# Grouped-query attention on one core: new planner constants, a reordered start, a shared last product

## The chip, the cores and the metric

The kernel runs on one core of a Trainium2 chip. The metric is the device time of one execution in microseconds, as the median of several runs. Five engines work side by side on a core: TensorE (PE in the profile, its weight loads PEld), VectorE (DVE), ScalarE (ACT), GpSimd (POOL) and SyncE (SP), which here only issues DMAs. Each engine takes its own instructions in order and waits on semaphores for the others.

## The reference

For each of 8 batches and 8 query heads, with 2 heads of keys and values (4 query heads share one), 1024 positions and 64 features:

```python
scores = scale * np.matmul(q_group, k_group.transpose(0, 1, 3, 2))
scores_max = np.max(scores, axis=-1, keepdims=True)
attn = np.exp(scores - scores_max)
attn = attn / (np.sum(attn, axis=-1, keepdims=True) + 1e-08)
output[:, q_start:q_end, :, :] = np.matmul(attn, v_group)
```

That is 64 jobs (a batch and a query head each), every one with 1024 x 1024 exponentials.

## The kernel before

**The work of a job.** The scores are made transposed, keys on the partitions. A job has 8 chunks of 128 keys; a chunk is a pair of matmuls (L522) into one PSUM slot of 128 x 1024 floats. There are three such slots (`sps`), each of two banks. The two matmuls of a pair use different halves of the rows of the array, and which key block goes with which half is why each turned k (`kt`) has a second plane with its halves swapped. From the slot the exponential goes to SBUF in bf16, by one of two ways:

- ScalarE takes the chunk with one ACTIVATE (L532, tile `pt`): 384 of the 512 chunks.
- VectorE takes it with an approximation in integer arithmetic: `yt` (L543, one pass over PSUM per chunk), and then for two chunks together `zt` (L550), `et` (L557) and a product (L566). For all jobs but the last two, `et` and `zt` both enter the next product (so such a chunk costs TensorE one more matmul per output piece); for the last two they are added (L571). This is a "chain"; 128 chunks make 64 of them.

The second product (L584) has 8 pieces per job, each of 128 queries, and accumulates 8 to 10 matmuls of 128 x 65 in PSUM; column 65 is the sum of the row, since v has a column of ones. Seven pieces share a bank (`PB = 7`), then VectorE takes the reciprocal of the sums (`rec`, L630) and multiplies (L633, tile `ost`), and SP stores whole jobs (L642). The last job is different: its chunks are accumulated as they come (`pvl`, L605) into both banks of a spare slot, four pieces in each, and each half is normalized and stored by itself (`half`, L617; the first half's store is issued by SP, the second's by ScalarE).

**The order.** Nothing is ordered by hand. The class `Plan` simulates TensorE, ScalarE and VectorE with cost constants (`M_...`, in ns), and writes a list of events; the kernel emits its instructions in that order. Since each engine takes its instructions in order, the plan decides only the order, not the times. The rules that matter here:

- `pick_d` (L88): VectorE may take at most `MXD = 2` chunks of a job, of the job in hand or the next two whose q is there.
- A score for ScalarE (kind "A") is emitted when ScalarE's planned work ahead (`runway`) is about to run out (`slack <= M_GAP`), or earlier, when a second slot is free or TensorE is at scores anyway and the runway is under `M_RUNWAY`. At most two are queued.
- Otherwise TensorE does `GRAIN = 3` matmuls of the second product at a time, and then decides again. Changing between scores and the second product costs `M_SWITCH`.
- In score mode TensorE may wait up to `M_WAIT` for a slot to come free rather than switch.
- Loads and turns of q, k and v, and the stores, are put into the event list at fixed distances from the planned times.

**The start (L412 to L454).** SP loads k of the first pair of heads and then v, ScalarE's queue loads q, GpSimd casts the q of the next jobs to bf16 in DRAM. TensorE runs 6 matmuls of 512 columns on zeros (`dummy`). k is cast by VectorE (L433), q by ScalarE (L434); TensorE turns k (four matmuls), then q (four), then the swapped k (eight, L445). VectorE copies the first block of k out (L450), ScalarE all of q (L451), VectorE the rest of k (L452) and the swapped plane (L453). The first score needs L450 and L451.

**Buffers.** `pt` has 32 buffers. So that the reuse of a buffer needs no wait of its own, every twelfth exponential is made to wait for the exponential 15 before it (L534 to L537).

Of the kernel before, what the change touches and what calls it, by code (L numbers as in the profile page):

```python
# [8 lines left out]


M_START = 5450
M_SWAP = 1200
M_Q1 = 3500
M_QSTEP = 2700
M_WARM = 7000
M_FILL = 12000
M_DUMMY = 110
M_SEE = 51
M_PAIR = 226
M_PTAIL = 205  # L20
M_SWITCH = 92
M_MM = 33.5
M_PVTAIL = 180
M_ACT = 905
M_ATAIL = 135
M_FIX = 76
M_DTAIL = 83
M_DEP = 34
M_D1 = 1.042
M_D2 = 0.521  # L30
M_D4 = 0.261
M_REC = 115
M_GAP = 60
M_RUNWAY = 1500
M_BACK = 2500
M_WAIT = 200
STEP = 10
INF = float("inf")
PB = 7
NPIECE = 8  # L40
GRAIN = 3
MXD = 2
TAIL = 2
STEPS = (("zh", M_D4), ("two", M_D4), ("mul", M_D2), ("add", M_D2))


class Plan:


    def __init__(self, nj, npt, nct, nyt):  # L50
        self.nj, self.npt, self.nct, self.nyt = nj, npt, nct, nyt
        self.ev = []
        self.spare = None
        self.mms = [8] * nj

        self.last = (nj - 1) * NPIECE
        self.groups = [(i, min(i + PB, self.last)) for i in range(0, self.last, PB)]
        self.groups += [(self.last, self.last + 4), (self.last + 4, self.last + 8)]
        self.group_of = [g for g, (lo, hi) in enumerate(self.groups) for _ in range(lo, hi)]
        self.run()  # L60

    def run(self):
        nj, ev = self.nj, self.ev
# [23 lines left out]

        def pick_d():  # L88
            for j in range(a, min(nj, a + 3)):
                if todo[j] and dcount[j] < MXD and qready[j] <= tP:  # L90
                    return j
            return None

        while pc < last or steps or norms:
# [12 lines left out]
            if tD == t:  # L107
# [27 lines left out]
                else:  # L135
# [10 lines left out]
                    if best:  # L146
                        at = max(t, dend + M_DEP) if best[0] else t
                        ch = best[2]
                        if ch is None:
                            _, _, lo, hi = norms.pop(0)  # L150
                            ev.append((t, "norm", (lo, hi), None, None))
                            end = at + M_FIX + 64 * (hi - lo) * M_D1
                            out_free[group_of[lo] % 2] = end + M_DTAIL + M_SEE
                            dlast = None
                        else:
                            n = len(ch["pairs"])
                            kind, rate = ch["steps"][ch["at"]]
                            ev.append((t, kind, None, ch["id"], n))
                            end = at + M_FIX + 1024 * n * rate
                            ch["at"] += 1  # L160
                            dlast = (ch["id"], ch["at"])
                            if ch["at"] == len(ch["steps"]):
                                chains.remove(ch)
                                for j, c in ch["pairs"]:
                                    p_ready[j][c] = end + M_DTAIL + M_SEE
# [82 lines left out]
            elif (  # L248
# [14 lines left out]
                ev.append((tP, "pvl", c, len(steps), None))  # L263
                tP += NPIECE * M_MM
                if not steps:
                    norms.append((tP + M_PVTAIL - 100, "rec", last, last + 4))
                    norms.append((tP + M_PVTAIL, "rec", last + 4, last + 8))
            elif t < M_FILL and pc == 0 and done == 0:
                ev.append((tP, "dummy", None, None, None))
                tP += M_DUMMY  # L270
# [13 lines left out]
def kernel(  # L284
# [28 lines left out]
    NPT = 32  # L313
# [99 lines left out]
    b16 = {x: kvp.tile([128, NH, 2 * D], BF16, name=f"{x}16") for x in "kq"}  # L413
    kt[(0, 0)] = ktp.tile([128, 2, HS], BF16, name="kt")
    qt[0] = qp.tile([128, 1, HS], BF16, name="qt")
    nc.sync.dma_start(out=f32["k"], in_=rows(k[0, 0], True))
    nc.scalar.dma_start(out=f32["q"], in_=rows(q[0, 0], True))
    load_v(0, 0)
    cast_q(1)
    make_identity(nc, ident)  # L420
    cast_q(2)
# [7 lines left out]
                ops[1][:, 0:cols], lhsT=warm[:, 0:128], rhs=warm[:, 0:cols], start=True, stop=True  # L429
            )  # L430

    dummy(6, HS)
    nc.vector.tensor_copy(out=b16["k"], in_=f32["k"])  # L433
    nc.scalar.activation(out=b16["q"], in_=f32["q"], func=AF.Copy)  # L434
    turned = {"k": new_slot(2)[:, 0, :], "q": new_slot(1)[:, 0, :]}
    for x in "kq":
        for c in range(NH):
            nc.tensor.matmul(  # L438
                turned[x][:, c * 128 : (c + 1) * 128],
                lhsT=b16[x][:, c, :], rhs=ident, start=True, stop=True,  # L440
            )
    for c in range(NH):
        for half in range(2):
            lo = half * D
            nc.tensor.matmul(  # L445
                ops[0][lo : lo + D, c * 128 : (c + 1) * 128],
                lhsT=b16["k"][:, c, D - lo : 2 * D - lo], rhs=ident, start=True, stop=True,
            )
    k0 = kt[(0, 0)]
    nc.vector.tensor_copy(out=k0[:, 0, 0:128], in_=turned["k"][:, 0:128])  # L450
    nc.scalar.activation(out=qt[0][:, 0, :], in_=turned["q"], func=AF.Copy)  # L451
    nc.vector.tensor_copy(out=k0[:, 0, 128:HS], in_=turned["k"][:, 128:HS])  # L452
    nc.vector.tensor_copy(out=k0[:, 1, :], in_=ops[0])  # L453
    turn_q(1)  # L454
    ev = list(plan.ev)
    n = len(ev)
# [15 lines left out]
    for x in [e for e in plan.ev if e[1] == "norm"]:  # L472
        lo, hi = x[2]
        for j in range(NJ - 1):
            if lo < (j + 1) * NPIECE <= hi:
                ev.append((x[0] + 700, "store", None, j, None))
        if lo >= plan.last:
            ev.append((x[0] + 1, "half", (lo, hi), None, None))
    order = {id(e): i for i, e in enumerate(ev)}
    ev.sort(key=lambda e: (e[0], order[id(e)]))  # L480

# [17 lines left out]
    for when, kind, x, j, c in ev:  # L499
# [14 lines left out]
        elif kind == "score":  # L514
# [4 lines left out]
            for half in range(2):  # L519
# [6 lines left out]
                    start=True,  # L526
                    stop=True,
                )
        elif kind == "act":
            p = pp.tile([128, 2, HS], BF16, name="pt")  # L530
            pt[(j, c)] = p
            exps.append(nc.scalar.activation(out=p, in_=where_s[(j, c)], func=AF.Exp, scale=scale))  # L532

            if len(exps) % 12 == 0 and len(exps) > 16:  # L534
                tc.add_manual_dep(
                    exps[-1].ins, exps[-16].ins.name, Sync, reason="buffers written before"
                )  # L537
        elif kind == "dpass":
            ch, i = j
# [72 lines left out]
                    )  # L612
        elif kind == "half":
            b, h = divmod(NJ - 1, H)
            lo, hi = x
            i = (lo - plan.last) // 2
            (nc.scalar if i else nc.sync).dma_start(  # L617
                out=rows(out[b, h])[:, i : i + 2],
                in_=ost[:, lo % RING : lo % RING + 4, :].rearrange("p (s two) d -> p s (two d)", two=2),
            )  # L620
        elif kind in ("rec", "norm"):
            lo, hi = x
            n = hi - lo
            o = ops[plan.group_of[lo] % 2]
            if lo >= plan.last:
                o = sps[plan.spare][:, (lo - plan.last) // 4, :]
            o = o[:, 0 : n * (D + 1)].rearrange("p (s d) -> p s d", d=D + 1)
            if kind == "rec":
                rec = rp.tile([128, PB], FP32, name="rec")
                nc.vector.reciprocal(out=rec[:, 0:n], in_=o[:, :, D])  # L630
            else:
                r = lo % RING
                nc.vector.tensor_tensor(  # L633
                    out=ost[:, r : r + n, :],
                    in0=o[:, :, 0:D],
                    in1=rec[:, 0:n].unsqueeze(2).to_broadcast([128, n, D]),
                    op=ALU.mult,
                )
        elif kind == "store":
            b, h = divmod(j, H)  # L640
            r = j * NPIECE % RING
# [35 lines left out]
```

The softmax here doesn't subtract the row's maximum and nothing guards it: scores larger than these inputs give would overflow.

## Time and profile before

| what | value |
|---|---|
| median of 6 runs | 366.65 us (365.76 to 368.26) |
| the profiled execution | 367.02 us |
| its span, first to last instruction | 365.2 us |
| TensorE / VectorE / ScalarE / GpSimd busy | 346.1 / 351.6 / 355.1 / 50.9 us |
| granted TensorE clock | 1.000 |
| exponentials on ScalarE, L532 | 384, 352.6 us busy |
| passes on VectorE over PSUM, L543 | 128, 155.7 us busy |
| matmuls of scores, L522 / of the second product, L584 | 1024 / 5024 |
| DMA, mean | 123 GB/s |

The profiled execution lies 0.37 us over the median, and 1.8 us of its time lie outside its span. A busy time counts each instruction from its start to its last write, and on ScalarE and VectorE one starts before the one ahead has ended; so a mean per instruction (1.10 us for an exponential) is more than what an instruction adds, which is the distance from start to start. On TensorE a pair of scores shows up as 0.384 us each, though the two run together.

### The profile page before, as it was taken

To read this page: it belongs to the slowest core of one execution; us is meant where nothing else is said; L and a number is where in the kernel's file an instruction comes from. 1 tells how busy PE (TensorE), PEld (TensorE's weight loads), DVE (VectorE), ACT (ScalarE), POOL (GpSimd) and SP (SyncE) were. 2 spreads that over 40 slices of the span, in tenths; PEclk is the share of its full clock that TensorE was granted. 3 is DMA by queue.
4 is the path that set the end of the run, shared out by engine and by line. 5 is a ranking of instruction groups with operands and counts; after the bars stand their busy time and mean duration, and the time that the engine had idled before them with its cause. 6 is when DMAs were issued, how large, how long until landed. Compare 5 with 4: busy or idle time off the path is not lost.

```text
span 365.2 us, 13795 instructions
## 1 busy us (share of the span) xinstructions
PE 346.1 (95%) x6155; PEld 220.4 (60%) x6155; DVE 351.6 (96%) x476; ACT 355.1 (97%) x387; POOL 50.9 (14%) x100
## 2 busy tenths in 40 slices
PE   6899999999999999999999999999999999999995
PEld 3466666666666666666656666655666656666664
DVE  3999999999999999999999999999999999999993
ACT  4999999999999999999999999999999999999994
POOL 3112021021211112021111112102111111211000
PEclk9999999999999999999999999999999999999999
DMA  5544768568647665857669576669686548754223
GB/s 154 92 102 115 133 118 147 131 117 162 117 89 155 124 145 92 171 100 132 149 103 157 105 140 138 120 145 117 110 158 114 139 85 170 131 120 91 70 59 88
DMA packets 89164, 44.81 MB, mean 123 GB/s; under 512 B 45488, under 2 KB 87345, under 8 KB 87857
## 3 DMA queue, kind: packets, MB, share of 16 engines
q1 hardware_dynamic: 86192, 33.31, 39.8%
q0 software_dynamic: 2496, 10.23, 21.8%
q8 instruction: 48, 0.79, 1.0%
q10 hardware_dynamic: 416, 0.39, 0.4%
q14 instruction: 12, 0.09, 0.1%
HBM read 25.17 MB, written 27.00 MB: 143 GB/s over the span
## 4 chain that ended last, share of the span: by engine, by line
ACT 56%; DVE 37%; PE 3%; DMA 1%; issue 1%
ACT pt L532 56%; DVE yt L543 16%; DVE zt L566 8%; DVE zt L550 5%; DVE ost L633 4%; DVE et L557 4%; PE sp L522 1%; DMA k<-in_k_dram 1%; DVE rec L630 1%; PE ops L584 1%; PE sp L605 1%; PE sp L438 0%; PE ops L428 0%; ACT qt L451 0%; DVE k L433 0%
## 5 line engine op out<-in xcount | busy, mean ns | idle before, releaser
L532 ACT ACTIVATE pt<-sp 128x1024 bf16<-128x1024 f32 x384 | 352.6, 1101 | 1.0 <-PE sp L522 0.7
L522 PE MATMUL sp<-qt,kt 64*128 64x512 bf16 x1024 | 173.3, 384 | 12.3 <-ACT pt L532 6.9
L584 PE MATMUL ops<-va,pt 128*128 128x65 bf16 x3024 | 184.6, 194 | 0.0
L584 PEld LDWEIGHTS <-pt 128*128 128x128 bf16 x3024 | 135.8, 97 | 43.2 <-issue 43.2
L543 DVE TENSOR_SCALAR yt<-sp 128x1024 uint16<-128x1024 f32 x128 | 155.7, 1217 | 2.3 <-PE sp L522 1.9
L584 PE MATMUL ops<-va,zt 128*128 128x65 bf16 x1008 | 124.4, 194 | 0.0
L584 PE MATMUL ops<-va,et 128*128 128x65 bf16 x992 | 120.3, 194 | 0.0
L584 PEld LDWEIGHTS <-et 128*128 128x128 bf16 x992 | 80.3, 98 | 26.0 <-issue 26.0
L584 PEld LDWEIGHTS <-zt 128*128 128x128 bf16 x1008 | 83.2, 97 | 6.9 <-issue 6.9
L522 PEld LDWEIGHTS <-kt 64*128 64x128 bf16 x1024 | 47.4, 93 | 58.0 <-issue 36.9
L566 DVE TENSOR_TENSOR zt<-yt,zt 128x2048 bf16<-128x2048 bf16 x64 | 78.0, 1219 | 0.0
L359 POOL DMA_DIRECT2D qd<-in_q_dram x63 | 32.5, 516 | 214.8 <-PE sp L522 208.6
L550 DVE TENSOR_SCALAR zt<-yt 128x2048 uint16<-128x2048 uint16 x64 | 46.4, 724 | 0.1
L633 DVE TENSOR_TENSOR ost<-ops,rec 128x448 f32<-128x448 f32 x72 | 44.2, 614 | 0.0
L557 DVE TENSOR_SCALAR et<-yt 128x2048 uint16<-128x2048 uint16 x64 | 43.2, 675 | 0.0
L367 POOL DMA_DIRECT2D kd<-in_k_dram x15 | 7.3, 487 | 64.9 <-PE sp L522 60.1
L630 DVE RECIPROCAL rec<-ops 128x7 f32<-128x7 f32 x72 | 14.1, 196 | 1.4 <-PE ops L584 1.3
L384 POOL CAST va<-vs 128x512 bf16<-128x512 f32 x16 | 10.6, 662 | 0.3 <-DMA vs<-in_v_dram 0.3
L428 PE MATMUL ops<-warm 128*128 128x128 bf16 (+1 forms) x27 | 4.7, 328 | 1.2 <-DVE warm L351 1.2
L428 PEld LDWEIGHTS <-warm 128*128 128x128 bf16 x27 | 2.1, 114 | 3.8 <-issue 2.6
L433 DVE CAST k<-k 128x512 bf16<-128x512 f32 x1 | 0.4, 426 | 3.2 <-DMA k<-in_k_dram 3.2
L434 ACT ACTIVATE q<-q 128x512 bf16<-128x512 f32 x1 | 0.6, 629 | 2.3 <-DMA q<-in_q_dram 2.3
(26 smaller groups left out, 16.4 us busy)
## 6 DMA issues: line engine op xcount, KB each, us to landing
out_dram<-ost SPq DMA_DIRECT2D x63, 256.0 KB, 2.8
qd<-in_q_dram POOLq DMA_DIRECT2D x63, 128.0 KB, 3.4
vs<-in_v_dram SPq DMA_DIRECT2D x16, 256.0 KB, 3.4
kd<-in_k_dram POOLq DMA_DIRECT2D x15, 128.0 KB, 3.0
kt<-kt SPq DMA_DIRECT2D x30, 64.0 KB, 2.8
qt<-qd SPq DMA_TRANSPOSE x63, 3.9
q<-in_q_dram ACTq DMA_DIRECT2D x1, 256.0 KB, 4.0
k<-in_k_dram SPq DMA_DIRECT2D x1, 256.0 KB, 4.1
```

Of the source, the lines that this page charges most:

```text
L359: return nc.gpsimd.dma_start(out=t.rearrange("(a x) d -> a (x d)", x=4), in_=q[b, h].rearrange("(a x) d -> a (x d)", x=8),)
L367: return nc.gpsimd.dma_start(out=t.rearrange("(a x) d -> a (x d)", x=4), in_=k[b, g].rearrange("(a x) d -> a (x d)", x=8),)
L384: return nc.gpsimd.tensor_copy(out=va[:, b * G + g, :, :, 0:D], in_=vs.pop((b, g)).rearrange("p c (two d) -> p c two d", two=2),)
L522: now = nc.tensor.matmul(sps[x][:, half, :], lhsT=t[lo : lo + D, c // NH, ci % NH * 128 : (ci % NH + 1) * 128], rhs=qt[j][lo : lo + D, 0, ...
L532: exps.append(nc.scalar.activation(out=p, in_=where_s[(j, c)], func=AF.Exp, scale=scale))
L543: nc.vector.tensor_scalar(out=yt[ch][:, i, :, :], in0=where_s[c], scalar1=EXP_A, scalar2=EXP_B, op0=ALU.mult, op1=ALU.add,)
L550: nc.vector.tensor_scalar(out=zt[j][:, 0:c], in0=yt[j][:, 0:c], scalar1=0x7F, scalar2=0x3F00, op0=ALU.bitwise_and, op1=ALU.bitwise_or,)
L557: ins = nc.vector.tensor_scalar(out=et[j][:, 0:c], in0=yt[j][:, 0:c], scalar1=0x7F80, scalar2=None, op0=ALU.bitwise_and,)
L566: nc.vector.tensor_tensor(out=z, in0=yt[j].bitcast(BF16)[:, 0:c], in1=z, op=ALU.mult)
L584: nc.tensor.matmul(ops[plan.group_of[x] % 2][:, lo : lo + D + 1], lhsT=p[:, qs * 128 : (qs + 1) * 128], rhs=va[:, b * G + h // HPG, ci % N ...
L630: nc.vector.reciprocal(out=rec[:, 0:n], in_=o[:, :, D])
L633: nc.vector.tensor_tensor(out=ost[:, r : r + n, :], in0=o[:, :, 0:D], in1=rec[:, 0:n].unsqueeze(2).to_broadcast([128, n, D]), op=ALU.mult,)
```

## The change

- **Constants of the plan.** A matmul of the second product 33.5 to 31.2 ns, an exponential 905 to 917, its tail 135 to 107, a VectorE instruction's fixed part 76 to 66, its tail 83 to 80, the reciprocal 115 to 90, gap 60 to 90, runway 1500 to 2200, wait 200 to 300, and the start's (`M_START`, `M_SWAP`, `M_Q1`, `M_WARM`). `GRAIN` 3 to 1.
- **A third VectorE chunk.** The limit in `pick_d` is one higher for jobs 1 and 33 (`MORE = 32`).
- **The start.** k is loaded in two parts (first block, then three). v is loaded by SP only once ScalarE has cast the first half of q. Two more dummies. q is cast half by ScalarE, half by VectorE; the first block of k by VectorE, the rest by ScalarE. q is turned first, k after it, its first block to a bank of its own. ScalarE copies out 320 columns of the turned q, VectorE the other 192, after k's first block. The swapped k is made after the first score.
- **The wait on buffers.** Every 26th exponential waits for the one 5 before it.
- **The end.** The two halves of the last job become one group: one reciprocal of all 8 sums, then VectorE multiplies four pieces while ScalarE multiplies the other four, one ACTIVATE of 64 columns each. Stores as before.

The diff, cut to its core (the constants are above):

```diff
-        self.groups += [(self.last, self.last + 4), (self.last + 4, self.last + 8)]
+        self.groups += [(self.last, self.last + 8)]
...
-                if todo[j] and dcount[j] < MXD and qready[j] <= tP:
+                if todo[j] and dcount[j] < MXD + (j % MORE == 1) and qready[j] <= tP:
...
-                    norms.append((tP + M_PVTAIL - 100, "rec", last, last + 4))
-                    norms.append((tP + M_PVTAIL, "rec", last + 4, last + 8))
+                    norms.append((tP + M_PVTAIL, "rec", last, last + 8))
...
-    nc.sync.dma_start(out=f32["k"], in_=rows(k[0, 0], True))
+    k0, q0 = kt[(0, 0)], qt[0]
+    for c, n in ((0, 1), (1, NH - 1)):
+        nc.sync.dma_start(out=f32["k"][:, c : c + n], in_=rows(k[0, 0], True)[:, c : c + n])
     nc.scalar.dma_start(out=f32["q"], in_=rows(q[0, 0], True))
-    load_v(0, 0)
...
-    dummy(6, HS)
-    nc.vector.tensor_copy(out=b16["k"], in_=f32["k"])
-    nc.scalar.activation(out=b16["q"], in_=f32["q"], func=AF.Copy)
...
+    dummy(8, HS)
+    nc.vector.tensor_copy(out=b16["k"][:, 0:1], in_=f32["k"][:, 0:1])
+    ins = nc.scalar.activation(out=b16["q"][:, 0:2], in_=f32["q"][:, 0:2], func=AF.Copy)
+    nc.vector.tensor_copy(out=b16["q"][:, 2:NH], in_=f32["q"][:, 2:NH])
+    nc.scalar.activation(out=b16["k"][:, 1:NH], in_=f32["k"][:, 1:NH], func=AF.Copy)
+
+    tc.add_manual_dep(load_v(0, 0).ins, ins.ins.name, Sync, reason="loads in time, not sooner")
...
+    for c in range(NH):
+        turn("q", c)
+    for c in range(NH):
+        turn("k", c)
+    QS = 320
+    nc.scalar.activation(out=q0[:, 0, 0:QS], in_=turned["q"][:, 0:QS], func=AF.Copy)
+    nc.vector.tensor_copy(out=k0[:, 0, 0:128], in_=turned["k0"][:, 0:128])
+    nc.vector.tensor_copy(out=q0[:, 0, QS:HS], in_=turned["q"][:, QS:HS])
+    nc.vector.tensor_copy(out=k0[:, 0, 128:HS], in_=turned["k"][:, 128:HS])
...
+            if len(where_s) == 1:
+                swap_k0()
...
-            if len(exps) % 12 == 0 and len(exps) > 16:
+            if len(exps) % (NPT - 6) == 0:
                 tc.add_manual_dep(
-                    exps[-1].ins, exps[-16].ins.name, Sync, reason="buffers written before"
+                    exps[-1].ins, exps[-6].ins.name, Sync, reason="buffers written before"
                 )
...
+                if lo >= plan.last:
+                    for i in range(4):
+                        nc.scalar.activation(
+                            out=ost[:, r + 4 + i, :], in_=o2[:, 1, i, 0:D],
+                            func=AF.Copy, scale=rec[:, 4 + i : 5 + i],
+                        )
```

`swap_k0` holds the eight matmuls of L445 and the copy of L453.

## The prediction, made before the changed kernel ran

> **What bounds the kernel now.** I read the page's busy times first, then the chain that ended last and the costliest groups, then the timelines of both ends.
>
> ```profile
> PE 346.1 (95%) x6155; PEld 220.4 (60%) x6155; DVE 351.6 (96%) x476; ACT 355.1 (97%) x387; POOL 50.9 (14%) x100
> ...
> ACT 56%; DVE 37%; PE 3%; DMA 1%; issue 1%
> ...
> L532 ACT ACTIVATE pt<-sp 128x1024 bf16<-128x1024 f32 x384 | 352.6, 1101 | 1.0 <-PE sp L522 0.7
> ...
> L543 DVE TENSOR_SCALAR yt<-sp 128x1024 uint16<-128x1024 f32 x128 | 155.7, 1217 | 2.3 <-PE sp L522 1.9
> ```
>
> Three engines look full, and the chain changes between ScalarE and VectorE. ScalarE is the one that runs through: its 384 exponentials start at 7.75 us, the last ends at 360.66. So the time is start + 384 steps + end. A step is 352.9 / 384 = 0.918 us on average; single records stand 0.904 apart at best, and in the median. The excess of 0.014 x 383 = 5.5 us is waiting that the rows hide, for instructions overlap: 3.6 us of it are 29 steps of over 0.96, where a score came late.
>
> The start, ScalarE's timeline:
>
> ```profile
> 4.71 0.63 ACT L434 ACTIVATE q<-q 128x512 bf16<-128x512 f32 x1 [2.27 <-DMA q<-in_q_dram]
> 6.45 0.60 ACT L451 ACTIVATE qt<-sp 128x512 bf16<-128x512 f32 x1 [1.11 <-PE sp L438]
> 7.75 3.07 ACT L532 ACTIVATE pt<-sp 128x1024 bf16<-128x1024 f32 x3 [0.70 <-PE sp L522]
> ```
>
> From q's landing to the first exponential, 3.04 us.
>
> The end, VectorE's timeline:
>
> ```profile
> 351.53 1.22 DVE L543 TENSOR_SCALAR yt<-sp 128x1024 uint16<-128x1024 f32 x1
> 352.66 0.19 DVE L630 RECIPROCAL rec<-ops 128x7 f32<-128x7 f32 x1
> 352.78 0.70 DVE L550 TENSOR_SCALAR zt<-yt 128x2048 uint16<-128x2048 uint16 x1
> 353.39 0.62 DVE L633 TENSOR_TENSOR ost<-ops,rec 128x448 f32<-128x448 f32 x1
> 353.92 0.69 DVE L557 TENSOR_SCALAR et<-yt 128x2048 uint16<-128x2048 uint16 x1
> 354.52 1.22 DVE L566 TENSOR_TENSOR zt<-yt,zt 128x2048 bf16<-128x2048 bf16 x1
> 355.65 0.20 DVE L630 RECIPROCAL rec<-ops 128x7 f32<-128x7 f32 x1
> ...
> 361.18 0.18 DVE L630 RECIPROCAL rec<-sp 128x4 f32<-128x4 f32 x1 [1.45 <-PE sp L605]
> 361.40 0.42 DVE L633 TENSOR_TENSOR ost<-sp,rec 128x256 f32<-128x256 f32 x1
> 361.74 0.17 DVE L630 RECIPROCAL rec<-sp 128x4 f32<-128x4 f32 x1
> 361.94 0.42 DVE L633 TENSOR_TENSOR ost<-sp,rec 128x256 f32<-128x256 f32 x1
> ```
>
> Here the starts give what each instruction really adds: yt 1.13, rec 0.12, zt 0.61, norm 0.53, et 0.60, product 1.13. Times their counts: 128 x 1.13 + 64 x 2.34 + 72 x 0.65 + 2 x 1.13 = 344 us. From its first pass (8.18) to the end of the norm at 357.5 VectorE had 349 us for 343 of these: **about 6 us idle**, so it is nearly as full as ScalarE.
>
> TensorE, by starts: a pair of scores 0.227, a matmul of the second product 0.031, and each excursion into scores 0.19 more (0.089 going back, 0.099 coming). 512 x 0.227 + 5024 x 0.031 + 267 excursions x 0.19 = 323 us in 354: some 30 us of slack, in spite of "95%".
>
> **What the Trainium skill says.** (1) "TensorE: Matmul & The Clock Gate", Part 1: the array starts at half clock, and about 3.4 us of sustained work release it. The trace agrees: matmuls of 128 columns 0.106 apart at 6 us, 0.056 at 10.4; after the six dummies TensorE idled 1.45 us, and scores still ran slow at 9.5. (2) "ScalarE: Activation LUTs", Rules for kernel authors: about 0.3 us per ACTIVATE and 0.83 ns an element; in the trace 512 columns take 0.60 (under its 0.72), and exponentials in a row 0.904, so that most of the fixed part overlaps. (3) "DMA: Bandwidth & Descriptors", Anatomy of one DMA: about 2.0 us and bytes at 436 GB/s. k, q and v together would be 3.8 us (estimate), q and k alone 3.2; measured 4.0 and 4.1 for q and k. (4) "Perfetto Trace Analysis", Identifying Dependency Chains: an instruction that waits on several engines may get semaphore instructions ahead of it. The trace has 31 of 17 ns each on ScalarE at L532.
>
> **The start.** v out of the way: at most 0.6 us by the page's estimate, at least nothing; I take 0.35, q at 4.35. Then, in place of a cast of 0.63, four turns of k, four of q and a copy of 0.60: ScalarE casts half of q (0.63 - 256 x 0.83 ns = 0.42, to 4.77), TensorE turns q (4 x 0.106, the last written 0.31 after its start: 5.45) and the first block of k (5.6); VectorE copies this block (0.21 by L450's step, to 5.8) and 192 columns of q (0.36, to 6.15). ScalarE's 320 columns (0.44) lie beside that, as does its cast of k's rest (0.53 at about 4.8), if k's second part has landed by 5.0; later than that, q's copy behind it on ScalarE moves with it. The first score starts at 6.2 instead of 7.10. Its 0.65 to the first exponential stay 0.65 at half clock, 0.43 at full; eight dummies end at 1.19 + 8 x 0.427 = 4.6 and close the hole, so I take half of that: 6.75. **Gain 1.0; from 0.4 (no help from v, late k) to 1.4.** If the plan's first exponentials then meet a late second score (the swapped k, 4 x 0.107 on TensorE, now stands before it), up to 0.3 goes; I count 0, for the second score is needed only 0.9 after the first. VectorE gains little: the swapped plane is copied (0.69) at about 7.2, first pass near 8.0 (8.18 before).
>
> v's wait stands on SP; behind it is the first DMA-transpose of q, at 6.04 before, so at 4.8 it holds nobody. v lands at 4.8 + 0.4 + 3.4 = 8.6, its placing on GpSimd (0.62, at 8.91 before) is done by 9.3, and the first second-product matmul came at 16.70: 7 us of cover, hence nothing.
>
> **The third chunks.** Two exponentials fewer: 2 x 0.918 = **1.84**. VectorE: 2 x 1.13 + one more chain 2.34 = 4.6, into its 6 us idle. TensorE: 16 matmuls x 0.031 = 0.5, into its slack. Bounds: 0 if `pick_d` never finds VectorE ready, 1.84.
>
> **The buffer wait.** 31 become 14; a step with one is 16 ns longer (0.920), at times 0.1 when the score came late too. The exponential waited for started five steps back and ended 3.4 us ago: no stall for what is queued behind it on ScalarE. **0.25**, from 0.2 to 0.5.
>
> **The end.** One reciprocal from 361.18; VectorE's half is stored as before at 361.85. ScalarE's four start at 361.42. The price of one is between 0.10 (my estimate: 0.05 overhead of a step, 0.904 - 0.853, and 64 columns) and 0.35 (the page); 0.18 each gives 362.15 against 362.40. **0.25**, from 0.4 gain to 0.4 loss.
>
> **The plan's constants.** They add no instruction; they move the order. Nothing in the trace of before shows the new order, so I bound it: at best it removes the 3.6 us of late scores; at worst it makes them so many again or more. The plan's matmul time becomes what I measure (31), the VectorE instruction too (66 + 1024 x 1.042 = 1133 ns, measured 1.13); the exponential becomes the mean that contains the waits (917), above the 904 of ScalarE alone, which lets scores come late by 13 ns a step, against a gap raised by 30 and a longer runway. I take 0.
>
> **Given back.** Now VectorE: 343 + 4.6 = 348 from 8.0 ends its norms at 356 with no idle at all, and from its last norm to the end the work needs (last chain, its product, reciprocal, norm, store) about 4.5: 360 + idle. ScalarE: 6.75 + 382 x 0.918 + 4.3 = 361.7. Both ends come close, so each will sometimes wait for the other: I give back 0.6.
>
> **Sum.** -1.0 - 1.84 - 0.25 - 0.25 + 0.6 = -2.74. On the profiled 367.02: 364.3; this execution was 0.37 over the median, so **363.9**.
>
> **The rivals.**
> - **The plan fits, late scores go.** Another 2 to 3 us off; VectorE's floor (360 + 1.8 outside the span) allows it only with next to no idle. 361.9. For: 29 such steps. Against: VectorE is now full.
> - **VectorE takes over.** It keeps its 6 us idle and has 4.6 more: 360 + 6 + 1.8 - 0.37 = 367.4. For: chain at 37%. Against: much of its idle (1.2 us of it at the start) was for want of a score.
> - **It does not do what it says:** the third chunk isn't taken. Start, end and semaphores alone: 365.2.
> - **TensorE becomes the bound (slower).** With `GRAIN = 1` TensorE may leave the second product for a score after each matmul, where scores now go in twos and threes (88 runs of four, 74 of six matmuls). Each more excursion costs 0.19; the 30 us of slack are used up at some 420 instead of 267, and beyond that ScalarE waits. At 450, 0.19 x 183 = 35 us more: 4 to 5 beyond what the gains leave, 370.5. Against: longer runway and wait both favour long score runs.
>
> **How the numbers follow.** Forecast 42% (own range 362.6 to 365.2), plan fits 17%, VectorE 14%, not taken 14%, TensorE 13%. What a measurement of this kernel tells from no change is about 0.5%, 1.8 us: faster means under 364.8, slower over 368.5. Faster: 36 of the 42, 17, 4 of the 14: 0.57. Slower: 13 and 2 from VectorE's upper end: 0.15. Same: 0.28. The range leaves out TensorE and the bottom of "plan fits": 361.3 to 368.0.
>
> **What would show it.** First exponential near 6.75; 382 exponentials and 130 VectorE passes; 14 semaphores at L532; the last store issued about 0.25 sooner after the last product; the exponentials' step within 0.912 to 0.920; score excursions near 267. I am wrong if the mean step rises over 0.925, if the first exponential isn't under 7.35, or if VectorE's first pass is later than 8.2 and its idle grows.

## The result, and the profile after

The changed kernel takes 368.88 us in the median against 366.82 before: a ratio of 1.0052 (95% interval 1.0040 to 1.0063). Slower by half a per cent, where 363.9, faster by 0.8%, was forecast, and above the top of the range (368.0). The profiled execution took 370.12, 1.2 over the median and above the slowest of the other 19 (369.02); its span is 368.3.

The page of the changed kernel: busy times, chain, and the groups of the exponentials and of VectorE's passes over PSUM.

```profile
PE 349.2 (95%) x6177; PEld 221.8 (60%) x6177; DVE 355.2 (96%) x481; ACT 356.6 (97%) x390; POOL 51.2 (14%) x100
...
DVE 72%; ACT 18%; PE 8%; issue 1%; ACTq 0%
...
L550 ACT ACTIVATE pt<-sp 128x1024 bf16<-128x1024 f32 x382 | 353.0, 1064 | 4.3 <-PE sp L538 3.8
...
L561 DVE TENSOR_SCALAR yt<-sp 128x1024 uint16<-128x1024 f32 x130 | 158.0, 1216 | 2.0 <-PE sp L538 2.0
```

The shares of busy time are what they were. The chain is not: it has turned over, from 56% ScalarE and 37% VectorE to 18% and 72%. The plan did give two more chunks to VectorE (382 exponentials and 130 passes), and ScalarE is now seen to sit idle before exponentials for 4.3 us, most of it for want of a score (3.8), where it was 1.0.

The start, ScalarE's timeline:

```profile
3.89 0.42 ACT L436 ACTIVATE q<-q 128x256 bf16<-128x256 f32 x1 [1.46 <-DMA q<-in_q_dram]
...
6.78 1.94 ACT L550 ACTIVATE pt<-sp 128x1024 bf16<-128x1024 f32 x2 [1.09 <-PE sp L538]
```

The first exponential starts at 6.78, 0.97 sooner. The end, VectorE's timeline and then ScalarE's:

```profile
363.77 0.21 DVE L655 RECIPROCAL rec<-sp 128x8 f32<-128x8 f32 x1 [0.90 <-PE sp L623]
364.02 0.42 DVE L658 TENSOR_TENSOR ost<-sp,rec 128x256 f32<-128x256 f32 x1
```

```profile
361.87 1.15 ACT L550 ACTIVATE pt<-sp 128x1024 bf16<-128x1024 f32 x1
364.52 0.93 ACT L666 ACTIVATE ost<-sp,rec 128x64 f32<-128x64 f32 x4 [1.50 <-DVE ost L658]
365.48 0.41 ACTq L634 DMA_DIRECT2D out_dram<-ost  x1
```

ScalarE's four do not lie beside VectorE's product: they begin when it has ended (364.02 + 0.42), and from the reciprocal to the last store's issue it is 1.71 us, 1.22 before.

Put together by ScalarE: start 0.97 sooner, two steps fewer, and still the last exponential ends at 363.02 (361.87 + 1.15) instead of 360.66. The mean step went from 0.9183 to 0.9320 us: 5.2 us of waiting were added in the middle. Some of this is peculiar to an execution 1.2 us over its median: `e11_old_end` below has the same order up to the end, was profiled at its own median, and has a mean step of 0.930, which makes 4.5 us. Where do they come from? The waits of TensorE for slots say it first. Before, and after:

```profile
PE sp L522 <- ACT pt L532: 6.9, 29, 0.5
...
PE sp L522 <- DVE yt L543: 1.8, 7, 0.4
```

```profile
PE sp L538 <- DVE yt L561: 5.0, 18, 1.0
...
PE sp L538 <- ACT pt L550: 3.8, 10, 0.5
```

TensorE, about to make a score, used to wait for ScalarE to leave a slot; now it waits for VectorE. A score for ScalarE that stands behind in TensorE's queue is then late too. And VectorE is late, in part for a reason that the prediction didn't see. The changed kernel's timeline, all engines, around one of the longest steps of the exponentials (from 336.4 to 338.2, 1.77 us):

```profile
334.31 1.48 DVE L568 TENSOR_SCALAR zt<-yt 128x2048 uint16<-128x2048 uint16 x1
...
334.61 0.63 POOL L385 CAST va<-vs 128x512 bf16<-128x512 f32 x1
335.70 0.39 PE L538 MATMUL sp<-qt,kt 64*128 64x512 bf16 x2
...
337.51 0.61 PE L538 MATMUL sp<-qt,kt 64*128 64x512 bf16 x4 [0.97 <-DVE yt L561]
```

This `zt` takes 1.48 us; its like take 0.69. In the middle of it GpSimd copies a v into place (L385, 0.63). The score after that waits 0.97 us for VectorE's slot. Going through the single records: in the changed kernel 7 of VectorE's instructions are 0.3 to 0.8 us longer than the median of their kind, each of them a `zt`, `et` or product with both ends in SBUF, each beside a copy of v, 4.3 us in sum. In the kernel before it was 9, 4.2 us in sum, for instance:

```profile
248.60 1.48 DVE L550 TENSOR_SCALAR zt<-yt 128x2048 uint16<-128x2048 uint16 x1
248.90 0.62 POOL L384 CAST va<-vs 128x512 bf16<-128x512 f32 x1
```

So the delays are not new; what they cost is. The steps of the exponentials show it. Take those over 0.96 us, and of each what is over 0.904. Steps that begin from 1 us before to 8 us after the start of one of the 9 lengthened instructions hold 1.6 us of this excess in the kernel before; those near one of the 7 in the changed kernel hold 3.6. Another 2.1 of the changed kernel lie in three steps between 25.9 and 31.6 us, to which the next section comes. What lies elsewhere is alike, 2.0 before and 1.9 after. (The rest of the 5.2 is in steps that are longer by a few ns: the median step went from 0.904 to 0.916.)

### The profile page after: what moved, and what is told of

Read it like the earlier page. It is cut to its first block, busy times and chain, and to the rows that moved or that the text cites. A ratio compares the mean times of both kernels' runs of the same rounds, so it can differ in the third digit from the quotient of the medians.

```text
span 368.3 us, 13833 instructions
## 1 busy us (share of the span) xinstructions
PE 349.2 (95%) x6177; PEld 221.8 (60%) x6177; DVE 355.2 (96%) x481; ACT 356.6 (97%) x390; POOL 51.2 (14%) x100
## 4 chain that ended last, share of the span: by engine, by line
DVE 72%; ACT 18%; PE 8%; issue 1%; ACTq 0%
DVE yt L561 30%; ACT pt L550 18%; DVE zt L584 15%; DVE zt L568 8%; DVE ost L658 8%; DVE et L575 8%; PE sp L538 3%; PE ops L602 3%; DVE rec L655 2%; PE ops L430 1%; PE sp L623 1%; ACT ost L666 0%; ACT qt L454 0%; PE sp L444 0%; DVE qt L456 0%
## 5 line engine op out<-in xcount | busy, mean ns | idle before, releaser
L602 PE MATMUL ops<-va,pt 128*128 128x65 bf16 x3008 | 181.5, 194 | 0.0
L602 PEld LDWEIGHTS <-pt 128*128 128x128 bf16 x3008 | 144.6, 98 | 33.5 <-issue 33.5
L561 DVE TENSOR_SCALAR yt<-sp 128x1024 uint16<-128x1024 f32 x130 | 158.0, 1216 | 2.0 <-PE sp L538 2.0
L602 PE MATMUL ops<-va,zt 128*128 128x65 bf16 x1024 | 137.5, 195 | 0.2 <-DVE zt L584 0.2
L602 PE MATMUL ops<-va,et 128*128 128x65 bf16 x1008 | 135.9, 195 | 0.0
L602 PEld LDWEIGHTS <-et 128*128 128x128 bf16 x1008 | 88.8, 98 | 23.5 <-issue 23.5
L602 PEld LDWEIGHTS <-zt 128*128 128x128 bf16 x1024 | 90.3, 98 | 14.6 <-issue 14.0
L575 DVE TENSOR_SCALAR et<-yt 128x2048 uint16<-128x2048 uint16 x65 | 44.9, 691 | 0.0
L385 POOL CAST va<-vs 128x512 bf16<-128x512 f32 x16 | 10.0, 623 | 4.7 <-DMA vs<-in_v_dram 4.7
L430 PE MATMUL ops<-warm 128*128 128x128 bf16 (+1 forms) x33 | 5.7, 320 | 1.2 <-DVE warm L352 1.2
```

What stands on the lines that cost most here:

```text
L385: return nc.gpsimd.tensor_copy(out=va[:, b * G + g, :, :, 0:D], in_=vs.pop((b, g)).rearrange("p c (two d) -> p c two d", two=2),)
L430: nc.tensor.matmul(ops[1][:, 0:cols], lhsT=warm[:, 0:128], rhs=warm[:, 0:cols], start=True, stop=True)
L561: nc.vector.tensor_scalar(out=yt[ch][:, i, :, :], in0=where_s[c], scalar1=EXP_A, scalar2=EXP_B, op0=ALU.mult, op1=ALU.add,)
L575: ins = nc.vector.tensor_scalar(out=et[j][:, 0:c], in0=yt[j][:, 0:c], scalar1=0x7F80, scalar2=None, op0=ALU.bitwise_and,)
L602: nc.tensor.matmul(ops[plan.group_of[x] % 2][:, lo : lo + D + 1], lhsT=p[:, qs * 128 : (qs + 1) * 128], rhs=va[:, b * G + h // HPG, ci % N ...
```

## The experiments

Times are medians; the kernel before, on the same chips beside them, had medians of 366.7 to 366.9. Most experiments change the time by less than 1%, and each ran on one of several chips, so differences of a few tenths between two of them are not certain. "Longer" is the sum, in the profiled execution, of what VectorE's instructions took over the median of their kind, where that was more than 0.1 us.

**The first theory was another: a hole.** In the profiled execution, TensorE's clock was halved from 23.7 to 30.5 us. Busy times by windows, changed kernel (the columns: length, TensorE, its weight loads, VectorE, ScalarE, GpSimd, granted clock, DMA share, GB/s):

```profile
20.00:22.00 2.00, 1.16 (x8) 0.28 (x7) 2.00 (x5) 2.00 (x3) 0.49 (x1) 1.00 0.68 101
22.00:24.00 2.00, 1.01 (x6) 0.30 (x6) 2.00 (x3) 2.00 (x3) 0.00 (x0) 0.92 0.56 164
24.00:26.00 2.00, 1.65 (x10) 0.65 (x10) 2.00 (x3) 2.00 (x4) 0.32 (x1) 0.50 0.29 66
26.00:28.00 2.00, 2.00 (x31) 1.47 (x29) 2.00 (x4) 1.27 (x3) 0.23 (x1) 0.50 0.39 66
```

From 20 to 25.8 us TensorE has only scores: the next second product, job 1's, starts at 25.81, after a VectorE chain that ends at 25.54. Then the clock falls, and ScalarE is idle for 0.73 of the last window. That looked like 2 us of the loss. Two experiments on it:

`e1_no_third`, the third chunks left out:

```diff
-                if todo[j] and dcount[j] < MXD + (j % MORE == 1) and qready[j] <= tP:
+                if todo[j] and dcount[j] < MXD and qready[j] <= tP:
```

> The changed kernel without the third VectorE chunks (384 exponentials again, the plan otherwise the new one). Theory 'hole': job 1's third chunk holds back job 1's second product, TensorE then has only scores from 20 to 25.8 us, its clock is halved from 23.7 to 30.5 and ScalarE loses 2 us there; without the third chunk the clock stays full, and against two more exponentials (1.84 us) 2 us come back: within 0.5 us of the changed kernel, mean step of the exponentials about 0.926. Rival 'VectorE is over-full': the 4.6 us of VectorE work are what is late; without them the mean step falls to 0.918 and the time to about 365.5.

Measured: 370.64, ratio to before 1.0094 (1.0068 to 1.0120). 1.8 us slower than the changed kernel, the opposite of both. The granted clock over its span is 0.996, there is no hole, the mean step is still 0.930, and TensorE's waits for VectorE's slots stay at 4.5 us. So taking the third chunks out doesn't bring the loss back. What they are worth this run can't tell, for its order has a fault of its own: "longer" is 2.7 here, only 2.0 us of the late steps' excess lie near these instructions, and 2.9 us lie in four steps of 1.5 to 1.8 us between 322 and 342 us, at full clock and with no lengthened instruction beside them. Why they are late was not looked into.

`e4_scores_twice`, the hole filled:

```diff
-            for half in range(2):
+            for half in (0, 1, 0, 1) if 23 <= len(where_s) <= 31 else (0, 1):
```

> The changed kernel, but TensorE makes the 23rd to 31st pairs of scores twice over (the same values into the same slot), which fills its hole from 20 to 25.8 us with work. Theory 'hole': the clock is not halved, the steps of the 23rd, 24th and 26th exponential fall from 1.86, 1.59, 1.32 to about 1.0, and 1.5 to 2 us come back, less up to 0.2 for each pair that ScalarE was waiting for: 367.0 to 367.8. Rival 'late work': the exponentials are late because job 1's product comes late and then crowds the scores, clock or no clock: 368.9 or more.

Measured: 369.26, ratio 1.0055 (1.0037 to 1.0073). The windows of this kernel:

```profile
22.00:24.00 2.00, 1.56 (x14) 0.63 (x12) 2.00 (x3) 1.79 (x3) 0.00 (x0) 1.00 0.55 164
...
26.00:28.00 2.00, 2.00 (x46) 1.54 (x46) 1.95 (x3) 2.00 (x3) 0.31 (x1) 1.00 0.48 74
```

The clock is full, and against the median nothing came back. In this trace a copy now meets a `zt` at 30.18 us and makes it 0.89 longer, which it did not in the changed kernel's, so that part of what the full clock gives is taken again. The executions of the changed kernel itself say the same: of the 19 behind its median, 11 had a granted clock of 1.000 and a median of 368.92, and 7 had 0.993 or 0.994 and 368.74. The hole is real in the execution that was profiled, and it is probably part of why that one was 1.2 us over its median; it does not explain the median. **This theory falls.** (The first window that I quote has 1.56 by x14 where it was 1.01 by x6: the doubled scores did run.)

**The start by itself.** `e3_start_only`: the kernel before with the new start's instructions and its four constants, all else as before.

```diff
-M_START = 5450
-M_SWAP = 1200
-M_Q1 = 3500
-M_WARM = 7000
+M_START = 5800
+M_SWAP = 1500
+M_Q1 = 3400
+M_WARM = 6400
...
+    k0, q0 = kt[(0, 0)], qt[0]
+    for c, n in ((0, 1), (1, NH - 1)):
+        nc.sync.dma_start(out=f32["k"][:, c : c + n], in_=rows(k[0, 0], True)[:, c : c + n])
...
```

> The kernel before with the new start alone (and the four start constants of the plan). Theory 'the start is a gain by itself': first exponential near 6.8 instead of 7.75, mean step as before (0.918): 365.9, 1.0 us under before. Rival 'a gain at the start is given back': an earlier ScalarE meets the same VectorE; then less than 0.4 us remains at the end.

Measured: 365.62, ratio 0.9966 (0.9948 to 0.9985); first exponential at 6.78, mean step 0.917. 1.1 us, all of it kept, and 1.0 against those executions of the kernel before, on the same chip, that had the same clock (11 at 0.999 or 1.000: 366.62). So the changed kernel loses 3.3 us against its own start.

**The copies of v.** `e5_v_dma`, the changed kernel without GpSimd's copies from the second pair of heads on; v comes by a DMA that converts to bf16 on the way, issued by GpSimd:

```diff
         elif kind == "lv":
-            load_v(*j)
+            b, g = j
+            for two in range(2):
+                ins = nc.gpsimd.dma_start(
+                    out=va[:, b * G + g, :, two, 0:D],
+                    in_=rows(v[b, g]).rearrange("p c (two d) -> p two c d", two=2)[:, two],
+                )
+                tc.add_manual_dep(ins.ins, now.ins.name, Sync, reason="loads in time, not sooner")
         elif kind == "pl":
-            place_v(*j)
+            if j == (0, 0):
+                place_v(*j)
```

> The changed kernel, but v of all later heads comes by a DMA from GpSimd's queue that casts to bf16 on the way, in two parts, in place of SP's load and GpSimd's copy; the plan's order is the same. In the changed kernel's trace 7 VectorE instructions are 0.3 to 0.8 us longer than their like, each beside a GpSimd copy of v, 4.3 us in sum. Theory 'no slack': the new plan times VectorE to the ns, so each such delay goes to the end; without the copies the mean step of the exponentials falls from 0.930 to about 0.920 and the time by 3 to 4 us, to 365 to 366. Rival 'exponential at 917': scores are ordered too late for a ScalarE that takes 0.904; then the copies don't matter, and less than 1 us comes back.

Measured: 365.66, ratio 0.9962 (0.9946 to 0.9979), 3.2 us under the changed kernel. The mean step is 0.918, "longer" has gone from 4.3 to 0.8, and the longest `zt` is 0.72. The page of this kernel:

```profile
ACT 96%; PE 2%; issue 1%; DVE 0%; ACTq 0%
...
L557 ACT ACTIVATE pt<-sp 128x1024 bf16<-128x1024 f32 x382 | 350.9, 1076 | 0.9 <-PE sp L545 0.9
```

ScalarE, VectorE and TensorE have the same instructions in the same order, and the chain is ScalarE's again. But the loads of v have changed too, not only the copies; the doubled copies below test the copies alone.

`e8_start_v_dma`: the same edit on e3, that is under the old plan.

> The kernel before with the new start, and v by casting DMAs as in e5, without GpSimd's copies. Theory 'no slack': here the plan leaves VectorE room, so the 2.6 us of longer VectorE instructions were mostly absorbed and little comes back, 0 to 1 us against the new start alone (365.6): 364.6 to 365.6. Rival: VectorE decides here too, then 2 us or more come back: under 363.6.

Measured: 365.96, ratio 0.9968 (0.9954 to 0.9983). "Longer" falls from 2.6 to 0.1 and nothing comes back: the old plan had absorbed it.

The other direction, each copy made twice, on both plans (`e9_copies_twice`, `e10_start_copies_twice`):

```diff
-        return nc.gpsimd.tensor_copy(
-            out=va[:, b * G + g, :, :, 0:D],
-            in_=vs.pop((b, g)).rearrange("p c (two d) -> p c two d", two=2),
-        )
+        t = vs.pop((b, g)).rearrange("p c (two d) -> p c two d", two=2)
+        for _ in range(2):
+            nc.gpsimd.tensor_copy(out=va[:, b * G + g, :, :, 0:D], in_=t)
```

> The changed kernel, with each of GpSimd's 16 copies of v made twice over (same values). If the copies lengthen VectorE's instructions and the new plan passes that on, twice the copies give about twice the loss: VectorE's longer instructions go from 4.3 us in sum to 7 to 9, and the time from 368.9 up by 2.5 to 5 us, to 371.4 to 374. If v's DMA helped in e5 for another reason (SP's queue, the loads), this costs less than 1 us.

> The kernel before with the new start, and each copy of v twice over. Theory 'the old plan leaves VectorE room': the same longer instructions on VectorE as in e9, but at most half of it in the time: 365.6 up by 0 to 2 us. Rival 'every VectorE delay counts in either plan': up by as much as in e9.

Measured: e9 370.69, ratio 1.0111 (1.0087 to 1.0135), "longer" 7.1; e10 366.08, ratio 0.9982 (0.9972 to 0.9991), "longer" 4.4. Under the new plan the doubled copies cost 1.8 us, between what my two explanations expected (10 of the 32 copies took 0.97 us or more instead of 0.62, so it may be that they waited instead of lengthening VectorE's instruction once more). Under the old one they cost 0.5. The late steps say where: near a lengthened instruction, counted as above, lie 6.5 us of excess in e9 and 1.7 in e10, elsewhere 2.1 and 1.3. TensorE's waits for slots of VectorE, e9 and then e10:

```profile
PE sp L537 <- DVE yt L560: 8.0, 22, 1.1
```

```profile
PE sp L535 <- DVE yt L558: 1.5, 5, 0.5
```

**The end.** `e2_own_tile`: ScalarE writes its four pieces to a tile of its own.

```diff
+    end = kvp.tile([128, 4, D], FP32, name="end")
...
-                            out=ost[:, r + 4 + i, :], in_=o2[:, 1, i, 0:D],
+                            out=end[:, i, :], in_=o2[:, 1, i, 0:D],
```

> The changed kernel, with ScalarE's four last pieces written to a tile of their own instead of the ring that VectorE's half is written to. Theory: ScalarE started its four at 364.52 only because it waited for VectorE's product (ends 364.44) through the shared tile; in a tile of its own it starts right after the reciprocal, at about 364.03, and the last store is issued 0.45 us sooner: 0.3 to 0.5 us faster than the changed kernel. Rival: it waits for something else (old stores, the PSUM slot), then nothing changes.

Measured: 368.67, ratio 1.0045 (1.0030 to 1.0060): not to be told from the changed kernel, and its timeline shows the wait unchanged:

```profile
362.67 0.42 DVE L659 TENSOR_TENSOR ost<-sp,rec 128x256 f32<-128x256 f32 x1
363.19 0.93 ACT L667 ACTIVATE end<-sp,rec 128x64 f32<-128x64 f32 x4 [1.51 <-DVE ost L659]
```

So it isn't the ring tile. What the two still have in common is the PSUM slot `sp` and the tile `rec`, which both read; that one of these is the reason isn't shown. `e11_old_end` takes the new end out:

```diff
-        self.groups += [(self.last, self.last + 8)]
+        self.groups += [(self.last, self.last + 4), (self.last + 4, self.last + 8)]
...
-                if lo >= plan.last:
-                    for i in range(4):
-                        nc.scalar.activation(
-                            out=ost[:, r + 4 + i, :], in_=o2[:, 1, i, 0:D],
-                            func=AF.Copy, scale=rec[:, 4 + i : 5 + i],
-                        )
```

> The changed kernel with the end of before (two reciprocals, two products on VectorE, ScalarE has no part). In the changed kernel ScalarE's four multiplications start when VectorE's product has ended (364.52 after 364.44), also with a tile of their own in e2; they share the PSUM slot that VectorE reads. From first reciprocal to the last store's issue the new end takes 1.71 us, the old 1.22. So this is 0.5 us faster than the changed kernel, 368.4; the rival (the new end saves something elsewhere, as the first reciprocal coming sooner) expects 368.9 or more.

Measured: 368.41, ratio 1.0048 (1.0029 to 1.0067): 0.47 under the changed kernel, as worked out, though the two intervals overlap. The traces agree: from the end of the last exponential to the end of the span it is 5.23 us in the changed kernel and 4.74 in e11.

**Both together.** `e12_v_dma_old_end`: e5 and e11.

> The changed kernel with v by casting DMAs and the end of before: e5's 365.66 less the 0.5 us of the end: 365.2, 0.45% under the kernel before. If it is not under 365.5 the end doesn't add up with it.

Measured: 365.15, ratio 0.9965 (0.9951 to 0.9980). This is the lowest median of the study, below both kernels, but by the ratios it is not to be told from e5 (0.9962), e3 (0.9966) or e8 (0.9968). In the traces the stretch after the last exponential is again 0.47 shorter than with the new end (5.23 against 5.70 in e5).

**Which constant takes the reserve away?** One at a time, or in two cases three that belong together:

```diff
e6_exp_905, on the changed kernel
-M_ACT = 917
+M_ACT = 905
e7_vector_slack, on the changed kernel
-M_FIX = 66
-M_DTAIL = 80
-M_REC = 90 
+M_FIX = 76
+M_DTAIL = 83
+M_REC = 115
e13_start_mm, on e3
-M_MM = 33.5
+M_MM = 31.2
e14_grain3, on the changed kernel
-GRAIN = 1
+GRAIN = 3
e15_old_gap, on the changed kernel
-M_GAP = 90
-M_RUNWAY = 2200
-M_WAIT = 300
+M_GAP = 60
+M_RUNWAY = 1500
+M_WAIT = 200
e16_mm335, on the changed kernel
-M_MM = 31.2
+M_MM = 33.5
```

> The changed kernel with one constant of the plan set back: an exponential at 905 instead of 917. Rival 'exponential at 917': the mean step falls to about 0.917 and the time to 364 to 365.5. Theory 'no slack': VectorE is still timed to the ns and still delayed by the copies, so the time stays within 1 us of the changed kernel's 368.9, though the exponentials are planned closer.

> The changed kernel with VectorE's constants set back (fixed part 76, tail 83, reciprocal 115), which gives VectorE 10 ns of slack per instruction in the plan, some 4 us in all. Theory 'no slack': the plan grows by less than what is no longer lost; TensorE's waits for slots that VectorE holds fall from 14 us to near 5, and the time to 366 to 367.5. Rival: as the changed kernel or slower, 368.9 to 371, for the plan just gets longer.

> The kernel before with the new start and one more constant of the plan changed: a matmul of the second product at 31.2 ns (measured) instead of 33.5. If the 2.3 ns per matmul (5024 of them, 11 us of TensorE time in the plan) were the reserve that absorbed the copies' delays in the old plan, this loses 2 us or more against the new start alone (365.6): over 367.6. If the reserve lies elsewhere, it stays within 0.7 us of 365.6.

> The changed kernel with the second product again planned three matmuls at a time (GRAIN 3). If deciding after each matmul made the order brittle, 2 us or more come back: under 366.9. If not, within 0.7 us of the changed kernel: 368.2 to 369.6.

> The changed kernel with gap, runway and wait set back (60, 1500, 200 for 90, 2200, 300). TensorE's waits in score mode for a slot that VectorE holds are 5.0 us in the changed kernel and 1.8 before; if the longer wait in score mode is what passes VectorE's delays on, 2 us or more come back: under 366.9. If not, 368.2 to 370.

> The changed kernel with the matmul of the second product set back to 33.5 ns. If that was the reserve, the exponentials' mean step falls from 0.930 to 0.920 or less, though the plan's own end may come later for want of TensorE; the time then is under 368. If not, the step stays at 0.927 or more.

| kernel | us | ratio to before (95%) | exponentials, mean step | longer, us |
|---|---|---|---|---|
| changed | 368.88 | 1.0052 (1.0040 to 1.0063) | 382, 0.932 | 4.3 |
| e6: exponential 905 | 367.82 | 1.0018 (1.0006 to 1.0031) | 383, 0.918 | 0.8 |
| e7: VectorE's constants back | 369.23 | 1.0057 (1.0035 to 1.0078) | 383, 0.923 | 5.6 |
| e14: grain 3 | 369.58 | 1.0065 (1.0042 to 1.0087) | 382, 0.932 | 3.5 |
| e15: gap, runway, wait back | 367.25 | 1.0009 (0.9997 to 1.0021) | 382, 0.926 | 1.9 |
| e16: matmul 33.5 | 376.81 | 1.0271 (1.0241 to 1.0301) | 382, 0.932 | 4.5 |
| e3: new start, old plan | 365.62 | 0.9966 (0.9948 to 0.9985) | 384, 0.917 | 2.6 |
| e13: e3, matmul 31.2 | 366.28 | 0.9985 (0.9975 to 0.9995) | 384, 0.919 | 3.5 |

None of those tried is it alone. (Not tried were ScalarE's tail, 135 to 107, the wait on buffers, and `M_SWITCH`, which the change also moves, from 92 to 93.) By what was expected, e7, e13, e14 and e16 came out as the alternative to a reserve in these constants; e6 and e15 fell between their two expectations. Slack on VectorE alone (e7) brought the exponentials closer, but what VectorE was spared came due at the end. VectorE and then ScalarE in e7:

```profile
360.07 1.17 DVE L589 TENSOR_TENSOR zt<-et,zt 128x2048 bf16<-128x2048 bf16 x1
```

```profile
349.72 10.28 ACT L550 ACTIVATE pt<-sp 128x1024 bf16<-128x1024 f32 x11
362.75 0.93 ACT L666 ACTIVATE ost<-sp,rec 128x64 f32<-128x64 f32 x4 [2.75 <-DVE ost L658]
```

The last exponential ends at 360.0, and VectorE's last chain only at 361.2; in the kernel before VectorE's was done at 356.99, 3.7 us ahead of ScalarE. The grain and the matmul's time, from either side, are no help (e13 loses 0.7 against e3 and e14 0.7 against the changed kernel, with intervals that overlap in both cases, and e16 makes it 8 us worse). Setting back gap, runway and wait (e15) or the exponential's time (e6) gave 1.6 and 1.1 us, but in both the copies also met other instructions than in the changed kernel ("longer" 1.9 and 0.8), so their gain can't be told from that luck. This stays open.

## Why the prediction was wrong

**The sum by its parts.** With e3 and e11 between before and after, the differences add up: start -1.1 (366.7 to 365.62), plan with third chunks and the buffer wait +2.8 (to 368.41), end +0.5 (to 368.88). The prediction had -1.0, -1.84 - 0.25 + 0.6 = -1.5, and -0.25. It is 4.3 us off in the middle and 0.7 at the end.

**The steps that failed** are two: "The plan's constants ... I take 0", the term that carries the loss, and the reading that made it look safe, "about 6 us idle", with what was built on it: "4.6, into its 6 us idle". I took the time that VectorE's typical steps didn't account for as free. The single records show that 4.2 us of the kernel before was instructions made longer by GpSimd's copies. So most of it was used up. Typical starts show what an instruction costs when nobody disturbs it; the difference to the real sum has to be looked up in the records, not called idle. What was left, about 2 us, is less than the 4.6 that the third chunks bring.

**The plan's constants, "I take 0".** From e3 to e11 it is +2.8; with the third chunks' two exponentials at their 1.84, constants, grain and buffer wait cost 4.6. (e1, the same without third chunks, is 5.0 over e3, 0.5 of it the end; but 2.9 of this are the four steps of its own.) I had bounded this term by the late scores of the kernel before, "so many again or more", 3.6 us, and then put it at nothing. What the runs show in its place: under the new plan the copies' delays reach the end. Four kernels show the interaction:

| | copies by GpSimd | casting DMA |
|---|---|---|
| new start, old plan | 365.62 (e3) | 365.96 (e8) |
| new start, new plan, old end | 368.41 (e11) | 365.15 (e12) |

With copies the new plan loses 2.8 us, without them it gains 0.8 by the medians, and nothing that is clear of noise by the ratios (0.9968 and 0.9965). So of the 4.3 us that the middle is off, some 3.6 are the copies' doing (3.1 by the ratios); the rest isn't explained. Under the new plan "longer" of 0.6, 4.3 and 7.1 us goes with 365.15, 368.41 and 370.2 (e9, less 0.5 for its end): about 0.6 to 0.9 us per us. Under the old plan 0.1, 2.6 and 4.4 go with 365.96, 365.62 and 366.08: next to nothing. That the new plan passes the delays on is shown by these and by the steps near the lengthened instructions; which part of the plan makes the difference stays open.

**The third chunks** (1.84) are not measured by themselves: e1 without them is 1.8 slower, but that this fits is luck, since four long steps of e1 alone make 2.9. Where the copies are gone they do bring nearly what was forecast: in the traces of e8 and e12 the exponentials last 352.5 and 350.9 us from the first start to the last end, 1.5 less. My "given back, 0.6" put VectorE's fullness at the wrong place and far too small. The rival "VectorE takes over" (367.4) named the right engine, and the chain of 72% VectorE is its mark; it lacked the copies and the end. The slower rival (370.5), more excursions of TensorE into scores, is refuted: by the records there are 248 runs of scores instead of 267.

**The start** was right in size: e3 gained 1.1 (1.0 predicted); first exponential 6.78 (6.75), VectorE's first pass 7.74 (8.0). Its parts differ: ScalarE's cast of q began at 3.89 instead of 4.35, and the first score came at 6.13 (6.2), from an earlier q and a longer wait for VectorE's copies. That the first exponential fits to 0.03 is luck. The 17 traces with the new start have it at 6.08 to 6.78; from the first score to it they take 0.43 in most and 0.65 in four, the changed kernel's among them, where I had taken the half between. My bound of 0.6 us for taking v out of the way didn't hold either: q landed 3.1 us after its issue instead of 4.0. The fit of the Trainium skill behind it ("DMA: Bandwidth & Descriptors", Anatomy of one DMA) is for DMAs that GpSimd issues, and these loads are issued by SyncE and ScalarE.

**The end** was wrong in its place: I priced ScalarE's four at 0.18 each from 361.42 on, "beside" VectorE's half. They take 0.20 from start to start, which is close, but come after VectorE's product: 0.47 lost where 0.25 was forecast as gained, a little outside the bound of 0.4 us loss.

**The buffer wait**: 16 semaphore instructions instead of 31 at the exponentials, 14 predicted. No experiment parts it from the constants.

**The chances** put 15% on slower. What I said would prove me wrong did: the mean step is over 0.925.

## What to carry to other kernels

When a plan places instructions by their undisturbed costs, look in the trace for the ones that took longer than their kind, and for what ran beside them, before calling the rest slack: this kernel, with three engines 95% to 97% busy, held 4.2 us of such lengthening, which the old order hid and the new one passed on. Test a tighter order together with the removal of its largest disturbance; here taking the copies away under the old order gained nothing, the tighter order alone lost 2.8 us, and the two together gained at most 0.8. And when two engines share a last step, see in the timeline whether they run at once.

## What was not expected of the hardware

- A copy on GpSimd (128 x 512, float32 to bf16, 0.62 us) lengthened VectorE instructions that read and write SBUF by up to 0.8 us (`zt` from 0.69 to 1.48), passes over PSUM not at all. The Trainium skill has this: "SBUF — State Buffer", Who interferes with whom, says that the two engines share a pair of ports, that VectorE's two-port modes and its instructions with two SBUF inputs contend with GpSimd there, and that the second to issue is blocked until the first is done. The traces agree on which instructions are lengthened. They don't show the order: the `zt` above started 0.30 us before the copy, and was the one that got longer, while the copy took its usual 0.63.
- The same stretch of work went with a halved clock in one execution and with the full clock in another. From 20 to 24 us, with scores alone, TensorE was busy for 2.2 us in the changed kernel's trace, and its clock was halved from 23.7 to 30.5; in e5 and e9, in the same order, it was busy for 1.9 and 2.1, and the clock stayed at 1.00.
- Four ACTIVATEs of 64 columns from PSUM, with a scale per row, started 0.20 us apart in a row, though the record of each is 0.31 us long.
